# A two-layer streaming encoder on one core: the first loads and copies laid out by hand, and the q, k, v products with two token blocks at a time

## The chip, the cores and the metric

The kernel runs on one core of one Trainium2 chip. The metric is the device time of one execution in microseconds (us), as a median over runs. The engines of the core are TensorE (PE in the profile: matrix products, PEld its weight loads), VectorE (DVE), ScalarE (ACT), GpSimd (POOL) and SyncE (SP), whose queue issues nearly all DMA transfers here.

## The reference

The input x has 2048 frames of 1024 channels, everything is float32. Layer 0 is a pooling mixer, layer 1 an attention layer that reads keys and values made from layer 0's output:

```python
h = rms_norm(x, a_norm)
u, z = split(h @ a_w_in)                       # 1024 + 1024 channels
pooled = trailing means of u over 2/4/8/16 frames (4 groups of 256 channels) - u
mixed = einsum(pooled, a_w_group) * a_scale    # a 256 x 256 map per group
x = x + (mixed * silu(z)) @ a_w_out
x = x + (p[0] @ ple_w[0]) * sigmoid(x @ ple_gate_w[0])
k, v = split(rms_norm(x, kv_norm) @ w_kv);  k = rms_norm per head
q, z = split(rms_norm(x, b_norm) @ b_w_in); q = rms_norm per head
a = strictly causal stick-breaking weights of q.k / 8 (16 heads of 64)
x = x + ((a @ v) * silu(z)) @ b_w_out
x = x + (p[1] @ ple_w[1]) * sigmoid(x @ ple_gate_w[1])
```

## The kernel before

Channels lie on the 128 partitions, frames along the free axis. The 2048 frames are four chunks (0 to 3) of 512; 1024 channels are 8 tiles (KT). A float32 value is kept as a high part `hi` (rounded to the type that TensorE multiplies) and a low part `lo` (the rest), and each product takes three matmuls: hi·hi, hi·lo, lo·hi. The high part is a copy by ScalarE, the low part a subtraction by VectorE or POOL (`split`, `put_split`).

**Weights.** All weights pass through one ring of 9 buffers of 512 KB (`UNITS`, tile `wpair`) in the order of a list, `plan`. `take` hands pieces to a product, `give_back` frees the oldest buffer and calls `pump`, which starts the next load. In chunk 0 a piece comes raw (tile `wraw`, ring `io` of 4 buffers), is split, and for most weights also written to DRAM as a finished pair (`once`); later chunks load that pair (`wpair<-once`, line 156). The map of a group is folded into the input weights once: `fold(g)` multiplies the transposed weights of u (tiles `uraw`, split into `uh` and `ul`) with the group's map (`wg`) in 48 matmuls and writes the result as `wf`.

**Order of the work.** The code is written in program order; a scheduler that simulates times sets the order of instructions on each engine and of DMA issues in SP's queue. `keep_in_program_order` fixes an instruction's place; in the attention part (`state["hold"]`) TensorE's are all fixed.

**The start** (end of the function). Issued in this order: the gain `g_a`, the load of `wg` for group 3, the four `uraw` loads of group 3, eight loads of x by turns on SP's and ScalarE's queue, the z weights, five small gains on ScalarE's queue; then `fold(3)`, then `prep(0)`, which splits x (tiles `xp`) and sums the squares of x per token with 32 one-column matmuls (tile `pst`).

**A chunk.** `mixer` (z and u products per group, pooling on VectorE, tiles `mp`), `out_steps` (output projection; `xr` is product plus residual), `gate_steps`, then the products for q, k and v (`kvq`, once for each half `b` of the heads, six per chunk) and z of layer 1. In `kvq` the tokens are on the output's partitions: a product has 4 blocks `j` of 128 tokens, each 8 steps `kt` of 3 matmuls, and needs all 8 weight pieces from its first block on. A PSUM bank (two with tag `psd`) collects a block; ScalarE empties it in `valued` (tile `vr`) or `keyed` (`qs`). For v the rows are also copied shifted by one frame (`vs<-vr`, `ve<-vr`), subtracted (`differences`) and written as `vd`; for q and k transposed parts are written as `qd` and `kd` at four places of the next product, through the list `lag`. Attention over the finished chunks runs between the steps of the next chunk's products; its tiles are `qa`, `qb`, `kk`, `vv`, `pp`, `at`.

Of the kernel before, what the change touches and what calls it, by code (L numbers as in the profile page):

```python
# [11 lines left out]
AF = mybir.ActivationFunctionType  # L12
ALU = mybir.AluOpType
# [18 lines left out]
def f(ap):  # L32
    return ap.bitcast(F32)
# [3 lines left out]
def trunk_kernel(ctx, tc, x, p, a_norm, wu_t, wz_a, w_group, a_scale, a_w_out, kv_norm, w_kv,  # L37
                 k_norm, b_norm, b_w_q, b_w_z, b_q_norm, b_w_out, ple_a, ple_b, gate_a, gate_b, out):
    nc = tc.nc
    V, A, G = nc.vector, nc.scalar, nc.gpsimd  # L40
    state = {"solo": True, "hold": False, "turn": 0, "lo": 0}

# [80 lines left out]
    def rsqrt_mean(out_ap, ss, n, tag):  # L123
# [3 lines left out]
        G.tensor_tensor(out=out_ap, in0=ms, in1=neghalf[:, 0:w], op=ALU.pow)  # L127

    def split(pr, src, lo):
        A.copy(out=pr[:, 0], in_=src)  # L130
        lo.tensor_tensor(out=pr[:, 1], in0=src, in1=f(pr[:, 0]), op=ALU.subtract)
# [4 lines left out]
    plan = []  # L136
    wq = {"out": 0, "back": 0, "cap": 1, "by": nc.scalar}
    held = deque()

    def put_split(pr, raw, kts, gain):  # L140
        if gain is None:
            A.copy(out=pr[:, 0], in_=raw)  # L142
            state["lo"] += 1
            (G if state["lo"] % 3 else V).tensor_tensor(out=pr[:, 1], in0=raw, in1=f(pr[:, 0]), op=ALU.subtract)  # L144
            return
        for i, kt in enumerate(kts):
            g = gain[:, kt : kt + 1]
            A.activation(out=pr[:, 0, i], in_=raw[:, i], func=AF.Identity, scale=g)
            V.scalar_tensor_tensor(out=pr[:, 1, i], in0=raw[:, i], scalar=g, in1=f(pr[:, 0, i]),
                                   op0=ALU.mult, op1=ALU.subtract)  # L150

    def unit(key, src, kts, n, gain, keep):
        kk = len(kts)
        pr = pool.tile([P, 2, kk, n], F32R, tag="wpair", name="wpair", bufs=UNITS)
        if key in once:
            nc.sync.dma_start(out=f(pr), in_=once[key])
            return pr, kts
        raw = io("wraw").rearrange("q (k n) -> q k n", k=kk)
        wq["by"].dma_start(out=raw, in_=src[:, kts[0] : kts[-1] + 1])
        put_split(pr, raw, kts, gain)  # L160
        if keep:
            once[key] = scratch(f"once{len(once)}", [P, 2, kk, n])
            nc.sync.dma_start(out=once[key], in_=f(pr))
        return pr, kts
# [102 lines left out]
    def fold_load(g):  # L267
        maps[g] = parts = {}
        raws = {}
        for h in range(2):  # L270
            for c in range(2):
                raws[c, h] = io("uraw")
                nc.sync.dma_start(out=raws[c, h], in_=wu_t[2 * g + c, :, h * W5 : (h + 1) * W5])
        for h in range(2):
            for c in range(2):
                hi, lo = ppt("uh", F32R), ppt("ul", F32R)
                A.copy(out=hi, in_=raws[c, h])
                V.tensor_tensor(out=lo, in0=raws[c, h], in1=f(hi), op=ALU.subtract)
                parts[c, h] = (hi, lo)

    def fold(g):
        parts = maps.pop(g)
        (wg, _), = take(1)
        for kts in PAIRS:
# [9 lines left out]
            for e, kt in enumerate(kts):  # L294
                gn = g_a[:, kt : kt + 1]
                A.activation(out=pr[:, 0, e], in_=ps[:, e], func=AF.Identity, scale=gn)
                V.scalar_tensor_tensor(out=pr[:, 1, e], in0=ps[:, e], scalar=gn, in1=f(pr[:, 0, e]),
                                       op0=ALU.mult, op1=ALU.subtract)
            assert plan[wq["out"]][0] == ("wf", g, kts) and wq["out"] - wq["back"] < UNITS
# [39 lines left out]

    first_x = []  # L340

    def load_first():
        for o in range(KT):
            xin = (qryt, ppt, keyt, valt)[(0, 2, 0, 3, 0, 2, 0, 3)[o]]("xin", F32)
            (nc.sync, nc.scalar)[o % 2].dma_start(out=xin, in_=x[o * P : (o + 1) * P, 0:W5])
            first_x.append(xin)

    def prep(s):
        ck = chunk[s]
        ck["x"] = []  # L350
        for o in range(KT):
            if s:
                xin = io("xin")
                nc.sync.dma_start(out=xin, in_=x[o * P : (o + 1) * P, s * W5 : (s + 1) * W5])
            else:
                xin = first_x[o]
            pr = pair("xp")
            split(pr, xin, G if s else V)
            ck["x"].append(pr)
            if s:  # L360
                gather_squares(ck, "acc1", o, xin)
            else:
                if o == KT - 1:
                    sums = turned()
                    for i in range(KT):
                        sq = tmp("sq")
                        A.activation(out=sq, in_=first_x[i], func=AF.Square)
                        for j in range(4):
                            tc.keep_in_program_order(
                                T.matmul(sums[:, 0, j : j + 1], sq[:, j * P : (j + 1) * P], ones,  # L370
                                         start=(i + j == 0), stop=(i == KT - 1 and j == 3)))
            yield
        r = token_norm(ck["acc1"], "x") if s else rooted(sums, "x")
        yield
        ck["rb1"] = bcast(r, "x")
        yield
# [10 lines left out]
    def pooled(s, o, ps, zr):  # L387
# [21 lines left out]
        pr = pair("mp")  # L409
        split(pr, po, G)  # L410
        ck["m"][o] = pr
# [80 lines left out]
    def settle():  # L492
        while late:
            late.pop(0)()

    def kvq(s, kind, b):
        ck = chunk[s]
        us = take(KT)
        for j in range(4):
            tk = slice(j * P, (j + 1) * P)  # L500
            ps = dense()
            for kt in range(KT):
                u = us[kt][0]
                for xh, wh in ((0, 0), (1, 0), (0, 1)):
                    T.matmul(ps, ck["x2"][kt][:, xh, tk], u[:, wh, 0], start=(kt == 0 and xh == wh),
                             stop=(kt == KT - 1 and wh == 1))
                    if j == 3 and wh:
                        give_back()
                    yield
                if lag and (j, kt) in ((1, 2), (1, 5), (2, 1), (2, 4)):  # L510
                    lag.pop(0)()
            if "r2" not in ck:
                ck["r2"] = token_norm(ck["acc2"], "y")
            rj = ck["r2"][:, j : j + 1]
            settle()
            (valued if kind == "v" else keyed)(s, kind, b, j, ps, rj)

# [300 lines left out]

    nc.scalar.dma_start(out=g_a, in_=a_norm)
    pump()  # L820
    fold_load(3)
    load_first()
    wq["by"] = nc.sync
    wq["cap"] = UNITS
    pump()
    for dst, v in ((g_s, a_scale), (g_b, b_norm), (g_kv, kv_norm), (gs[:, 0:1], k_norm), (gs[:, 1:2], b_q_norm)):
        nc.scalar.dma_start(out=dst, in_=v)
    V.scalar_tensor_tensor(out=gqk, in0=gs[:, 1:2], scalar=HD ** -0.5, in1=gs[:, 0:1],
                           op0=ALU.mult, op1=ALU.mult)
    for _ in fold(3):  # L830
        pass
    for _ in prep(0):
        pass

    until((0, 0))
# [111 lines left out]
```

## Time and profile before

| what | value |
|---|---|
| median of 3 runs | 2834.18 us (2833.43 to 2836.98) |
| profiled execution | 2834.65 us, of which the span from first to last instruction is 2832.9 us |
| TensorE busy | 2733.4 us (96%), mean granted clock 0.985 |
| VectorE, ScalarE, POOL busy | 65%, 45%, 31% |
| DMA | 643.37 MB, mean 227 GB/s |

In the lists of waits below, a line gives the engine that waited, its tile and line, what it waited for, and then the sum in us, the number of times and the longest. In a list by time, a line gives start and length in us, engine, line, operation, `out<-in`, shapes and count; brackets give the idle time before it and what ended it. In a list of windows, a line gives the window, its length, the busy time of each engine with its instructions, the granted clock of TensorE, the DMA engines' busy share and GB/s.

### The profile page before, as it was taken

Reading aid. Unit: us, or ns where it says so; the run is one execution under the profiler, and the core shown is the slowest. Engines: PE = TensorE matmul, PEld = TensorE weight load, DVE = VectorE, ACT = ScalarE, POOL = GpSimd, SP = SyncE. Lnnn points to the kernel's source line nnn. Section 1 sums busy time; section 2 is a strip of 40 time slices with the busy share of each in tenths; the row PEclk is TensorE's granted clock in tenths of the full one; section 3 lists DMA queues with packets and bytes.
Section 4 is the critical chain, followed back from the end, with each engine's and each line's share of the span. In section 5 each row is a group of like instructions: output and inputs, shape, how many; then the busy total and the mean of one; then the engine's idle time right before and its main releaser. Section 6 shows DMA issues by size and latency. Waiting matters only on the chain.

```text
span 2832.9 us, 38130 instructions
## 1 busy us (share of the span) xinstructions
PE 2733.4 (96%) x13400; PEld 2246.7 (79%) x13400; DVE 1840.4 (65%) x2369; ACT 1271.2 (45%) x2496; POOL 870.4 (31%) x699
## 2 busy tenths in 40 slices
PE   7999979999988999999999999999999999999999
PEld 7888857878866787788778888888888888888777
DVE  5645444655334686766458888776777877777872
ACT  4435542344433445545344456554454444444441
POOL 1354422455423354553213434221211101111002
PEclk8999989999999999999999999999999999999999
DMA  5647899556788966786776444778577667656535
GB/s 213 222 142 278 309 323 307 178 176 208 257 258 282 334 224 218 235 308 228 244 251 219 146 147 153 241 225 274 177 230 240 244 213 255 207 198 230 176 127 185
DMA packets 306123, 643.37 MB, mean 227 GB/s; under 512 B 48646, under 2 KB 81414, under 8 KB 305932
## 3 DMA queue, kind: packets, MB, share of 16 engines
q1 hardware_dynamic: 304348, 639.62, 68.1%
q8 instruction: 105, 1.72, 0.3%
q10 hardware_dynamic: 1584, 1.33, 0.1%
q14 instruction: 86, 0.70, 0.1%
HBM read 471.43 MB, written 161.02 MB: 223 GB/s over the span
## 4 chain that ended last, share of the span: by engine, by line
PE 79%; DMA 8%; DVE 5%; SPq 2%; issue 2%; ACT 2%; POOL 2%; ACTq 0%; DVEq 0%; POOLq 0%
PE psd L46 55%; PE psl L46 8%; PE pso L46 7%; PE psa L50 7%; DMA wpair<-once 3%; DVE pp L743 2%; DVE at L760 1%; DMA wraw<-in_b_w_q_dram 1%; PE pst L50 1%; DMA xin<-in_x_dram 1%; DMA vs<-vr 1%; POOL wpair L144 1%; PE pst L46 1%; SPq L523 1%; DMA kraw<-in_b_w_out_dram 1%
## 5 line engine op out<-in xcount | busy, mean ns | idle before, releaser
L743 DVE TENSOR_TENSOR_SCAN pp<-pp,floor 128x512 f32<-128x512 f32 (+3 forms) x640 | 774.7, 1210 | 34.5 <-ACT pp L739 33.6
L760 DVE TENSOR_TENSOR at<-psa,at 128x512 fp32r<-128x512 f32 (+3 forms) x640 | 387.1, 605 | 431.9 <-ACT at L758 429.6
L46 PE MATMUL psd<-wpair,x 128*128 128x512 f32 x2304 | 620.5, 403 | 38.8 <-DMA wpair<-once 22.7
L758 ACT CAST at<-psa 128x512 fp32r<-128x512 f32 (+3 forms) x640 | 333.6, 521 | 690.6 <-PE psa L50 665.4
L46 PE MATMUL psd<-x,wpair 128*128 128x512 f32 x2304 | 599.3, 393 | 3.5 <-ACT sg L481 3.5
L46 PEld LDWEIGHTS psd<-wpair,x 128*128 128x128 f32 x2304 | 426.0, 191 | 139.6 <-DMA wpair<-once 38.0
L46 PEld LDWEIGHTS psd<-x,wpair 128*128 128x128 f32 x2304 | 427.0, 188 | 92.5 <-ACT sg L481 4.6
L46 PE MATMUL psd<-xp,wpair 128*128 128x512 f32 x1536 | 391.8, 396 | 6.4 <-DMA wpair<-once 6.4
L50 PE MATMUL psa<-ident,pp 128*128 128x128 f32 x2176 | 347.2, 274 | 17.4 <-DVE pp L743 6.6
L46 PE MATMUL pso<-at,vv 128*128 128x512 f32 (+3 forms) x1280 | 361.5, 364 | 0.2 <-DVE at L760 0.2
L50 PEld LDWEIGHTS psa<-ident,pp 128*128 128x128 f32 x2176 | 274.8, 141 | 104.8 <-DVE at L760 12.2
L739 ACT ACTIVATE pp<-psl 128x512 f32<-128x512 f32 (+3 forms) x640 | 344.6, 538 | 12.5 <-PE psl L46 9.2
L46 PEld LDWEIGHTS psd<-xp,wpair 128*128 128x128 f32 x1536 | 287.4, 190 | 66.3 <-DMA wpair<-once 7.7
L46 PE MATMUL psl<-kk,qa 128*128 128x512 f32 (+3 forms) x640 | 284.4, 444 | 2.9 <-DMA kk<-kd 2.9
L46 PEld LDWEIGHTS pso<-at,vv 128*128 128x128 f32 x1280 | 240.7, 189 | 54.0 <-DVE at L760 0.5
L46 PE MATMUL psl<-kk,qb 128*128 128x512 f32 (+3 forms) x640 | 234.2, 366 | 0.0
L46 PE MATMUL psd<-og,wpair 128*128 128x512 f32 x744 | 202.6, 395 | 2.0 <-DVE os L773 2.0
L46 PE MATMUL psd<-mp,wpair 128*128 128x512 f32 x768 | 196.9, 398 | 7.5 <-DVE xr L449 7.5
L144 POOL TENSOR_TENSOR wpair<-wraw,wpair 128x512 fp32r<-128x512 f32 x101 | 148.4, 1474 | 128.3 <-ACT wpair L142 127.9
L46 PEld LDWEIGHTS psd<-mp,wpair 128*128 128x128 f32 x768 | 145.0, 192 | 38.2 <-DVE xr L449 8.3
L46 PEld LDWEIGHTS psd<-og,wpair 128*128 128x128 f32 x744 | 137.5, 188 | 31.5 <-DVE os L773 2.6
L474 POOL TENSOR_TENSOR xj<-x 128x512 f32<-128x512 f32 x64 | 101.7, 1594 | 135.5 <-DVE sg L485 129.6
(112 smaller groups left out, 2747.4 us busy)
## 6 DMA issues: line engine op xcount, KB each, us to landing
wpair<-once SPq DMA_DIRECT2D x384, 512.0 KB
once<-wpair SPq DMA_DIRECT2D x80, 512.0 KB
kk<-kd SPq DMA_DIRECT2D x160, 256.0 KB
vv<-vd SPq DMA_DIRECT2D x160, 256.0 KB
wpair<-wf SPq DMA_DIRECT2D x48, 512.0 KB
once<-kp SPq DMA_DIRECT2D x36, 512.0 KB
wraw<-in_a_w_out_dram SPq DMA_DIRECT2D x64, 256.0 KB
wraw<-in_gate_a_dram SPq DMA_DIRECT2D x64, 256.0 KB
```

Source lines behind the costliest of these rows:

```text
L46: return held_in_order(nc.tensor.matmul(*a, **k))
L50: return held_in_order(nc.tensor.transpose(*a, **k))
L144: (G if state["lo"] % 3 else V).tensor_tensor(out=pr[:, 1], in0=raw, in1=f(pr[:, 0]), op=ALU.subtract)
L474: G.tensor_tensor(out=xj, in0=f(x1[o][:, 0]), in1=f(x1[o][:, 1]), op=ALU.add)
L523: nc.sync.dma_start(out=vs[lo + 1 : hi + 1], in_=vr[lo:hi])
L739: A.activation(out=pp[:, r0:], in_=ps[:, :w], func=AF.Sigmoid, scale=-1.0)
L743: V.tensor_tensor_scan(out=pp[:, r0:][:, ::-1], data0=pp[:, r0:][:, ::-1], data1=least, initial=1.0 if st["diag"] else st["carry"][j], op0 ...
L758: A.copy(out=at[:, 0, cs], in_=pt[:, cs])
L760: return lambda: V.tensor_tensor(out=at[:, 1, cs], in0=pt[:, cs], in1=f(at[:, 0, cs]), op=ALU.subtract)
```

## The change

1. **The start** is a function of its own, `boot`. The first two of four map pieces are loaded first, on two queues (into `t4` tiles `u`, two pieces each, not the `io` ring), then `wg`, the other two pieces, then `g_a` and x; seven of x's eight loads and the five small gains are on SP's queue. Copies and subtractions of the start are fixed in program order (`booted`); the splits of the first z weights wait in a list `later` and are called at set places. Half of x's low parts go from VectorE to POOL. The whole fold of group 3 is issued in pieces of 12 or 13 matmuls between the copies, and the sums of squares come after 56 of the xp products.
2. **`kvq`** walks the list `STEPS`: blocks 0 and 1 as before, then block 2 alone for four steps, then blocks 3 and 2 by turns, then block 3's last four steps. The weight piece of a step is still given back by block 3.
3. **`pooled`**: the low parts of `mp` for channel tiles 0 and 1 (the group that comes last) are made by VectorE instead of POOL.

```diff
-            A.activation(out=pr[:, 0, i], in_=raw[:, i], func=AF.Identity, scale=g)
...
+            booted(A.activation(out=pr[:, 0, i], in_=raw[:, i], func=AF.Identity, scale=g))
...
-        wq["by"].dma_start(out=raw, in_=src[:, kts[0] : kts[-1] + 1])
-        put_split(pr, raw, kts, gain)
+        booted(nc.sync.dma_start(out=raw, in_=src[:, kts[0] : kts[-1] + 1]))
+
+        def finish():
+            put_split(pr, raw, kts, gain)
+            if keep:
+                nc.sync.dma_start(out=once[key], in_=f(pr))
+
...
+        if state["boot"]:
+            later.append(finish)
+        else:
+            finish()
...
     def load_first():
+        two = [t4("u0") for _ in range(2)]
+        for h in range(2):
+            for c in range(2):
+                first_u[c, h] = f(two[h])[:, c]
+                ins = (nc.scalar if c else nc.sync).dma_start(out=first_u[c, h],
+                                                             in_=wu_t[6 + c, :, h * W5 : (h + 1) * W5])
+                if not c:
+                    booted(ins)
+            if h == 0:
+                pump()
+        nc.scalar.dma_start(out=g_a, in_=a_norm)
...
-            (nc.sync, nc.scalar)[o % 2].dma_start(out=xin, in_=x[o * P : (o + 1) * P, 0:W5])
+            ins = (nc.scalar if o == 1 else nc.sync).dma_start(out=xin, in_=x[o * P : (o + 1) * P, 0:W5])
...
+    def cast_first(os):
+        for o in os:
+            pr = pair("xp")
+            booted(A.copy(out=pr[:, 0], in_=first_x[o]))
+            booted((G if o % 2 else V).tensor_tensor(out=pr[:, 1], in0=first_x[o], in1=f(pr[:, 0]), op=ALU.subtract))
...
+    def boot():
+        load_first()
+        later.pop(0)()
+        fold_split(3, first_u)
+        wq["cap"] = UNITS
+        pump()
+        run = fold(3)
...
+        cast_first(range(4))
+        folds(13)
+        cast_first(range(4, KT))
+        folds(12)
+        later.pop(0)()
+        folds(12)
+        later.pop(0)()
+        later.pop(0)()
+        folds(12)
+        later.pop(0)()
+        sum_first()
...
-        split(pr, po, G)
+        split(pr, po, G if o > 1 else V)
...
+    STEPS = [(j, kt) for j in range(2) for kt in range(KT)]
+    STEPS += [(2, 0), (2, 1), (2, 2), (2, 3), (3, 0), (2, 4), (3, 1), (2, 5), (3, 2), (2, 6), (3, 3), (2, 7)]
+    STEPS += [(3, kt) for kt in range(4, KT)]
+
     def kvq(s, kind, b):
...
-        for j in range(4):
+        banks = {}
+        for j, kt in STEPS:
             tk = slice(j * P, (j + 1) * P)
-            ps = dense()
-            for kt in range(KT):
-                u = us[kt][0]
...
+            if kt == 0:
+                banks[j] = dense()
+            u = us[kt][0]
+            for xh, wh in ((0, 0), (1, 0), (0, 1)):
+                T.matmul(banks[j], ck["x2"][kt][:, xh, tk], u[:, wh, 0], start=(kt == 0 and xh == wh),
+                         stop=(kt == KT - 1 and wh == 1))
+                if j == 3 and wh:
+                    give_back()
+                yield
```

How the rows of two engines change at the start. First SP's queue, from its first row on, before (xin is x, uraw a map piece, wraw of in_wz_a a z weight piece):

```order
L345 DMA xin<-in_x_dram 128x512 x2
L273 DMA uraw<-in_wu_t_dram 128x512 x3
L345 DMA xin<-in_x_dram 128x512 x2
L273 DMA uraw<-in_wu_t_dram 128x512
L159 DMA wraw<-in_wz_a_dram 128x512 x4
```

and after (u_379 and u_380 are the two tiles of the map pieces):

```order
L363 DMA u_379<-in_wu_t_dram 128x512
L164 DMA wraw<-in_a_w_group_dram 128x512
L363 DMA u_380<-in_wu_t_dram 128x512
L372 DMA xin<-in_x_dram 128x512 x7
L164 DMA wraw<-in_wz_a_dram 128x512 x4
L421 DMA gains<-in_a_scale_dram 128x8
```

The map pieces and wg now stand ahead of x (the other two pieces are the first two rows of ScalarE's queue), and the gains behind the z weights. ScalarE's copies at the start, before (uh is the high part of a map piece, wpair<-psd the folded weights, sq the squares):

```order
L277 CAST uh<-uraw 128x512
L827 DMA gains<-in_kv_norm_dram 128x8
L827 DMA gs<-in_k_norm_dram 128x1
L827 DMA gs<-in_b_q_norm_dram 128x1
L130 CAST xp<-xin 128x512 x8
L367 ACTIVATE sq<-xin 128x512 x6
L277 CAST uh<-uraw 128x512
L148 ACTIVATE wpair<-wraw,g_a 128x256 x8
L296 ACTIVATE wpair<-psd,g_a 128x256 x7
```

and after:

```order
L147 CAST wpair<-wraw 128x512
L293 CAST uh<-u_379 128x512 x2
L293 CAST uh<-u_380 128x512 x2
L380 CAST xp<-xin 128x512 x4
L312 ACTIVATE wpair<-psd,g_a 128x256 x2
L380 CAST xp<-xin 128x512 x4
L312 ACTIVATE wpair<-psd,g_a 128x256 x2
L153 ACTIVATE wpair<-wraw,g_a 128x256 x2
L312 ACTIVATE wpair<-psd,g_a 128x256 x2
L153 ACTIVATE wpair<-wraw,g_a 128x256 x4
L312 ACTIVATE wpair<-psd,g_a 128x256 x2
L153 ACTIVATE wpair<-wraw,g_a 128x256 x2
```

The fourth map piece moved from behind x and the squares to the front, and the folded and z weights are copied by turns. On TensorE, behind the fold of group 3, before:

```order
L46 MATMUL psd<-wpair,ul 128x256
L46 MATMUL pst<-ones,sq 128x1 x32
L46 MATMUL psd<-xp,wpair 128x512 x22
L50 MATMUL pst<-ident,r 128x128 x4
L46 MATMUL psd<-xp,wpair 128x512 x70
```

and after:

```order
L46 MATMUL psd<-wpair,uh 128x256
L46 MATMUL psd<-xp,wpair 128x512 x56
L46 MATMUL pst<-ones,sq 128x1 x32
L46 MATMUL psd<-xp,wpair 128x512 x22
L50 MATMUL pst<-ident,r 128x128 x4
L46 MATMUL psd<-xp,wpair 128x512 x18
```

The sums of squares stand behind 56 of the 96 xp matmuls (before, behind four that stood within the fold). The second place is SP's queue in chunk 1 at the end of the first v product, where the loads for the next q product (`wpair<-once`) stand. Before:

```order
L571 DMA kd_7_316<-hl 64x2x512
L540 DMA vd_0_359<-vv 128x8x128
L523 DMA vs<-vr 112x512
L523 DMA vs<-vr 15x512
L530 DMA ve_0_367<-vr 1x512
L156 DMA wpair<-once_3573 128x1024
L156 DMA wpair<-once_3583 128x1024
L156 DMA wpair<-once_3593 128x1024
L156 DMA wpair<-once_3603 128x1024
```

and after:

```order
L643 DMA kd_7_316<-hl 64x2x512
L161 DMA wpair<-once_3558 128x1024
L161 DMA wpair<-once_3571 128x1024
L161 DMA wpair<-once_3584 128x1024
L612 DMA vd_0_359<-vv 128x8x128
L595 DMA vs<-vr 112x512
L595 DMA vs<-vr 15x512
L602 DMA ve_0_367<-vr 1x512
L161 DMA wpair<-once_3609 128x1024
```

Three of the eight loads moved ahead of vd, vs and ve (one more stands ahead of the four kd rows). TensorE's own rows are the same number in both, 13342.

107 lines of the change are left out of this document (52 added, 55 removed).

## The prediction

> **What bounds the kernel now.** I read the page first, then the list of waits of TensorE, then its gaps in order of time, and last what each gap waits for.
>
> ```profile
> span 2832.9 us, 38130 instructions
> PE 2733.4 (96%) x13400; PEld 2246.7 (79%) x13400; DVE 1840.4 (65%) x2369; ACT 1271.2 (45%) x2496; POOL 870.4 (31%) x699
> PE psd L46 <- DMA wpair<-once: 29.1, 28, 7.2
> PE psd L46 <- ACT uh L277: 14.2, 2, 8.1
> PE psd L46 <- ACT wpair L148: 13.6, 5, 6.1
> ```
>
> TensorE works 96% of the span, so what can be won without touching its matmuls is its idle time, 2832.9 − 2733.4 = 99.5 us, and the time in which its clock is low. Three entries are weights that were late (29.1 and 13.6 us) or the first pieces of the map (14.2 us at the start). The stages with the late weights are the last parts of the chunks, where the q, k, v products run; one row per chunk (each engine's busy time, then granted clock, DMA share, GB/s):
>
> ```profile
> 350.00:490.00 140.00, 117.47 (x517) 92.77 (x516) 61.56 (x91) 51.35 (x92) 32.50 (x31) 0.90 0.95 315
> 805.00:945.00 140.00, 121.23 (x564) 95.88 (x563) 57.28 (x81) 53.42 (x109) 40.86 (x37) 0.94 0.85 281
> 1330.00:1470.00 140.00, 132.35 (x648) 104.82 (x647) 72.64 (x99) 59.18 (x119) 31.77 (x30) 0.99 0.75 238
> 1925.00:2065.00 140.00, 138.82 (x714) 114.70 (x712) 100.11 (x123) 67.30 (x134) 30.34 (x25) 1.00 0.66 217
> ```
>
> TensorE is idle 22.5, 18.8, 7.6 and 1.2 us there; the DMA engines are full in chunk 0, have 15% left in chunk 1 and 25% in chunk 2. So the price of late weights sits in chunks 0 and 1, and only chunk 0 has no room in its transfers.
>
> **Part 1, the start.** TensorE's order of time at the start, and what ScalarE and SP's queue do meanwhile:
>
> ```profile
> 8.14 0.79 PE L46 MATMUL psd<-wpair,uh 128*128 128x256 f32 x2 [8.14 <-ACT uh L277]
> 9.25 0.41 PE L46 MATMUL psd<-wpair,uh 128*128 128x256 f32 x1
> 9.46 0.41 PE L46 MATMUL psd<-wpair,ul 128*128 128x256 f32 x1
> 14.76 0.28 PE L46 MATMUL psd<-wpair,ul 128*128 128x256 f32 x1
> 14.88 0.28 PE L46 MATMUL psd<-wpair,uh 128*128 128x256 f32 x1
> 21.23 0.80 PE L46 MATMUL psd<-wpair,uh 128*128 128x256 f32 x2 [6.07 <-ACT uh L277]
> 26.00 11.64 PE L46 MATMUL pst<-ones,sq 128*128 128x1 f32 x64
> 37.49 7.29 PE L46 MATMUL psd<-xp,wpair 128*128 128x512 f32 x22
> 44.98 16.14 PE L46 MATMUL psd<-xp,wpair 128*128 128x512 f32 x70
> 60.95 0.28 PE L46 MATMUL psd<-wpair,uh 128*128 128x256 f32 x1
> 61.00:350.00 289.00, 289.00 (x1360) 1.00 0.66 232
> 13.28 4.26 ACT L130 CAST xp<-xin 128x512 fp32r<-128x512 f32 x8 [2.84 <-DMA gains<-in_a_scale_dram]
> 20.58 0.60 ACT L277 CAST uh<-uraw 128x512 fp32r<-128x512 f32 x1
> 21.09 2.50 ACT L148 ACTIVATE wpair<-wraw,g_a 128x256 fp32r<-128x256 f32 x6
> 9.87 12.39 SPq L159 DMA_DIRECT2D wraw<-in_wz_a_dram  x4
> GB/s 0 0 104 267 241 295 279 391 388 382 410 393 336 352 347 321 342 369 249 144 8 0 0 11 0 0 0 0 0 0 79 295 363 292 284 412 399 402 404 388
> ```
>
> The fold of group 3 (48 matmuls) stops after 25 for 6.07 us: its fourth raw piece was cast at 20.58, behind the eight casts of x (13.28 to 17.54) and the squares of x. The last row is the DMA rate from 0 to 30 us in slices of 0.75 us: nothing moves from 15.75 to 22.5, since the z weights (9.87, four issues in 12.39 us) wait for buffers. Both are order, not work.
>
> The common milestone is the first matmul of the next fold, at 60.95; ahead of it both versions have 48 fold matmuls, 96 of xp, 32 sums (64 records) and 4 transposes. After the change:
> - The first four transfers are two map pieces, wg and the third piece, 4 x 0.26 = 1.05 MB. The slices sum to 0.89 MB at 5.25 and 1.18 at 6.0, so they are there at 5.65; the casts of wg and of one piece (0.60 each) put the first matmul at 6.9.
> - ScalarE, by the order: wg, 4 pieces, 4 x, 2 wf, 4 x, 2 wf, then the first z piece. A 512-wide cast goes each 4.26 / 8 = 0.53, a 256-wide one each 2.50 / 6 = 0.42: 5.65 + 0.6 + 12 x 0.53 + 5 x 0.42 = 14.7. x is no limit: 3.4 MB are in by 12.
> - The fold: starts of matmuls lie 0.21 us apart at 9.25 and 0.12 at 14.76, so TensorE's clock was half for some 6.2 us. As before, 28 slow ones take 6.0 and 20 fast ones 2.4: end at 15.3. For the lo parts that VectorE and POOL make I add 0.7: xp starts at 16.0.
> - One xp matmul is (60.95 − 44.98) / 70 = 0.228. By the order 56, the sums, 22, transposes and 18: 16.0 + 12.8 + 11.5 (26.00 to 37.49) + 7.5 (37.49 to 44.98, with transposes) + 4.1 = 51.9.
>
> That is 60.95 − 51.9 = 9.0 us less. Low end 6: TensorE waits for the second to fourth z piece (their casts alternate with wf casts that wait for VectorE). High end 10.4: the clock opens after 3.2 us, as it did from 21.23 on. The Trainium skill (TensorE: Matmul & The Clock Gate, Part 1) says that the clock is full after about 3.4 us of sustained matmuls, whenever they begin; by it the fold ends some 1.3 us sooner and the sum is 1.3 us lower. The second burst agrees with it and the first does not, so I leave that outside the sum. From 61 to 350 us TensorE is busy without a gap (289.00 of 289.00), so the 9.0 us reach chunk 0's end; weights are fetched when TensorE gives a buffer back, so that distance moves along. The five gain loads leave ScalarE's queue (they held its casts 2.84 us) for SP's, behind the z weights; the first user of them comes after 60 us, so that is free. The DMA pause moves to nothing: the wf and once writes (8 x 0.5 MB) follow at once, and the next fold's pieces are behind them as before.
>
> **Part 2, two token blocks together.** Before, block 3 gave weights back at its steps, 9 to 16 of the 16 that blocks 2 and 3 take; now at steps 5, 7, 9, 11 and 13 to 16. The first comes 4 steps sooner, then 3, 2, 1, 0.
>
> ```profile
> 286.38 27.37 PE L46 MATMUL psd<-wpair,x 128*128 128x512 f32 x120
> 819.32 3.33 SPq L571 DMA_DIRECT2D kd<-hl  x4
> 822.75 0.70 SPq L540 DMA_DIRECT2D vd<-vv  x1
> 823.50 3.36 SPq L523 DMA_DIRECT2D vs<-vr  x2
> 827.43 4.06 SPq L156 DMA_DIRECT2D wpair<-once  x8
> 831.34 2.30 PE L46 MATMUL psd<-wpair,x 128*128 128x512 f32 x4 [7.20 <-DMA wpair<-once]
> 899.40 3.36 PE L46 MATMUL psd<-wpair,x 128*128 128x512 f32 x7 [5.11 <-DMA wpair<-once]
> PE psd L46 <- DMA wpair<-once: 20.9, 18, 7.2
> PE psd L46 <- DMA wpair<-once: 4.4, 9, 0.7
> ```
>
> A step is 3 matmuls of 27.37 / 120 = 0.228, 0.68 us, and about 0.85 where attention runs between: 2.7 to 3.4 us sooner. It works through SP's queue. The wait of 7.20 is no lack of bytes: eight weight loads stood behind vd and two vs copies and issued at 827.43. By the order three of them now stand ahead of vd, one ahead of kd: 827.43 − 822.75 = 4.7 us sooner.
> - Chunk 1 (the list of waits from 760 to 945 us, first of the two): 20.9 us. 7.20 loses 4.7; the one of 5.11 loses 3.4; the rest, 8.6 in sixteen small waits, lies mostly inside that advance, say 6.4: 14.5 at best. Loads that come sooner queue with other traffic at 0.85 share, so I take 9; ends 4 and 14.5.
> - Chunk 2 (the second, 1330 to 1470): 4.4 us in nine waits under 0.7. I take 3, ends 1 and 4.4. Chunk 3: nothing.
> - Chunk 0: 22.5 us, but at 0.95 share the room is 0.05 x 140 = 7 us. I take 3, ends 0 and 7.
> - Clock. After a long gap it is half until TensorE has run some time:
>
> ```profile
> 826.00:827.00 1.00, 0.00 (x0) 0.96 1.03 290
> 837.00:838.00 1.00, 1.00 (x6) 0.92 1.00 356
> 830.40 0.62 ACT L538 CAST vv<-vs 128x512 fp32r<-128x512 f32 x1 [6.19 <-POOL vs L535]
> 1064.88 2.03 POOL L131 TENSOR_TENSOR mp<-us,mp 128x512 fp32r<-128x512 f32 x1 [2.19 <-ACT mp L130]
> 1075.15 0.66 DVE L449 TENSOR_TENSOR xr<-psd,xr 128x512 f32<-128x512 f32 x1
> 1075.86 1.47 PE L46 MATMUL psd<-mp,wpair 128*128 128x512 f32 x3 [4.19 <-DVE xr L449]
> ```
>
>   It fell just before 827, where TensorE had stopped at 831.34 − 7.20 = 824.1, and came back just after 837: of the work from 831.34 on some 5.8 us ran at half, 2.9 us lost. If the gap of 5.11 costs as much, cutting both below 2.5 us wins 5.8 at best; I take 3, since I leave 2.5 of the one and 1.7 of the other.
> - New waits. A PSUM bank of the pair is wanted again 4 steps after its block ends (2.7 us) instead of 8 (5.5), and ScalarE, which empties it, can stand behind a vv cast for 6.19 us. I take 2 lost; ends 0 and 8.
>
> Sum: 9 + 3 + 3 + 3 − 2 = 16 gained.
>
> **Part 3, the low parts.** Eight subtractions (o of 0 and 1 in four chunks) go from POOL (2.03 in the row) to VectorE at about the 0.66 of a 512-wide one. No matmul waits for the POOL one: it ended at 1066.9, and the gap at 1075.86 is for the bank that the xr add frees, which stands behind VectorE's queue. So nothing is gained and one 0.6 is added there: 0.6 lost, ends 0 and 1.3.
>
> **Sum.** 2834.65 (the profiled execution, 0.5 above the median of 2834.18) − 9.0 − 16 + 0.6 = 2810.2; I say 2810.
>
> **Rivals.**
> - Traffic takes it back: loads start sooner but land as late, since chunk 0 is at 0.95 and chunk 1 in stretches at 1.0. Chunk 0 gives 0, chunk 1 gives 3, chunk 2 gives 1, clock 1, new waits −3, together 2: 2834.65 − 9 − 2 + 0.6 = 2824. For it speak the shares, against it the 7.20, which is an issue held back.
> - All of part 2 comes: 7 + 14.5 + 4.4 + 5.8 = 31.7, and 2834.65 − 9 − 31.7 + 0.6 = 2794.6. Against it again the shares.
> - The start's gain is lost: the pieces of the next fold come at about 58 as before, so TensorE waits for them: 2810 + 9 = 2819. Against it: SP has their loads ahead of more of the once writes than before.
> - Slower: ScalarE empties the banks late. Each spot costs 6.19 − 2.7 = 3.5 us, 2810 + 3.5 N; there are 2 spots in each of 24 products, and the kernel is slower by 0.2% from N = 9 (2841.5). For it the row at 830.40; against it, that is a stand of ScalarE while TensorE itself was stopped, and in chunk 3 no wait of that size is seen.
>
> **How the numbers follow.** The forecast 2810 (2800 to 2820 where no term reaches its end) has 0.62, traffic 0.18, all of part 2 0.08, the start lost 0.08, slower 0.04. The range 2796 to 2826 leaves out the slower case, most of the full gain and the tails of traffic. A measurement tells 0.2% (5.7 us) from no change: faster than 2828.5 is all of four cases but a tail of traffic, 0.91; same 0.05; slower 0.04.
>
> **What would show it.** Right: first matmul near 7, no idle time over 1 us until the xp products, next fold near 52; no wait of 7 us in chunk 1, weights' waits there about 10 us, chunk 0 still near 20. Wrong: waits of TensorE for ScalarE's vr or qs at L46, a late uh in the second fold, or the idle time of chunk 1 unchanged.

## The result and the profile after

The changed kernel takes 2811.41 us (median of four runs, 2806.34 to 2817.46), the kernel before 2834.18 (2833.43 to 2836.98): a ratio of 0.9919, with 95% between 0.9898 and 0.994, so 0.6 to 1.0% faster. The forecast was 2810 us. The profiled execution is the longest of the four, 2817.46 us with a span of 2815.7; by the two profiled executions the change wins 17.2 us, by the medians 22.8. Two executions lie far above all others, one of e2_kvq (3453.95 us) and one of the kernel before (15448.73 us), and enter no figure. From the page, as before:

```profile
span 2815.7 us, 38145 instructions
PE 2733.7 (97%) x13400; PEld 2249.9 (80%) x13400; DVE 1847.9 (66%) x2373; ACT 1272.0 (45%) x2496; POOL 863.9 (31%) x695
```

TensorE's busy time is what it was (2733.4); its idle time fell from 99.5 to 82.0 us, by 17.5, which covers the difference of the spans (17.2). Its list of waits shows where:

```profile
PE psd L46 <- DMA wpair<-once: 17.5, 20, 4.8
PE psd L46 <- ACT wpair L153: 14.0, 6, 9.3
PE psd L46 <- ACT uh L293: 7.5, 2, 7.0
PE psl L46 <- DMA kk<-kd: 3.0, 1, 3.0
```

The weights fetched by DMA went from 29.1 to 17.5 us, the map pieces of the start from 14.2 to 7.5; the weights copied by ScalarE stayed (13.6 to 14.0). No wait for vr or qs is in the list. The start, in TensorE's order of time:

```profile
7.02 0.79 PE L46 MATMUL psd<-wpair,uh 128*128 128x256 f32 x2 [7.02 <-ACT uh L293]
8.41 0.80 PE L46 MATMUL psd<-wpair,ul 128*128 128x256 f32 x2 [0.59 <-DVE ul L294]
14.80 0.28 PE L46 MATMUL psd<-wpair,ul 128*128 128x256 f32 x1
16.72 12.88 PE L46 MATMUL psd<-xp,wpair 128*128 128x512 f32 x56
29.44 11.64 PE L46 MATMUL pst<-ones,sq 128*128 128x1 f32 x64
40.94 7.30 PE L46 MATMUL psd<-xp,wpair 128*128 128x512 f32 x22
52.63 0.28 PE L46 MATMUL psd<-wpair,uh 128*128 128x256 f32 x1
```

The wait of 6.07 us within the fold is gone, the xp products begin at 16.72, and the next fold at 52.63 instead of 60.95. The DMA rate of these first 30 us, in slices of 0.75 us, has no empty stretch left (the old one, from 15.75 to 22.5 us, was nine slices long, with 11 GB/s in one of them):

```profile
GB/s 0 0 55 238 341 374 404 375 365 393 246 183 232 303 341 391 366 407 399 321 164 70 266 421 22 169 421 404 393 404 421 382 399 399 399 284 238 429 426 300
```

The four stretches with the q, k, v products, one row per chunk, shifted by 10 to 17 us to begin at the same work (length, then each engine's busy time, then granted clock, DMA share, GB/s):

```profile
340.00:480.00 140.00, 120.91 (x534) 94.45 (x533) 60.99 (x90) 52.17 (x92) 34.91 (x34) 0.91 0.95 309
793.00:933.00 140.00, 127.02 (x591) 102.01 (x590) 58.55 (x83) 54.91 (x111) 40.68 (x37) 0.94 0.88 289
1315.00:1455.00 140.00, 135.11 (x672) 109.30 (x672) 76.68 (x105) 62.15 (x123) 35.14 (x33) 0.99 0.77 245
1908.00:2048.00 140.00, 139.61 (x719) 115.60 (x717) 101.10 (x123) 66.81 (x134) 30.91 (x26) 1.00 0.65 210
```

TensorE is idle 19.1, 13.0, 4.9 and 0.4 us there, against 22.5, 18.8, 7.6 and 1.2. The DMA share rose in chunk 1 from 0.85 to 0.88, the rate from 281 to 289 GB/s: more bytes in the same 140 us. In chunk 1 the wait of 7.20 us is gone; first TensorE's stops of over 1 us between 800 and 900 us, then the rows of SP's queue that belong to them:

```profile
816.19 0.50 PE L46 MATMUL psd<-wpair,x 128*128 128x512 f32 x1 [3.15 <-DMA wpair<-once]
822.86 1.11 PE L46 MATMUL psd<-wpair,x 128*128 128x512 f32 x3 [2.07 <-DMA wpair<-once]
825.15 1.22 PE L46 MATMUL psd<-wpair,x 128*128 128x512 f32 x2 [1.18 <-DMA wpair<-once]
885.89 2.38 PE L46 MATMUL psd<-wpair,x 128*128 128x512 f32 x4 [4.76 <-DMA wpair<-once]
811.11 1.82 SPq L161 DMA_DIRECT2D wpair<-once  x3
813.02 0.38 SPq L612 DMA_DIRECT2D vd<-vv  x1
813.50 2.64 SPq L595 DMA_DIRECT2D vs<-vr  x2
816.70 2.72 SPq L161 DMA_DIRECT2D wpair<-once  x4
```

Of the eight loads that had issued together at 827.43, behind vd and two vs rows, three now issue at 811.11, ahead of them, and four at 816.70. The one stop of 7.20 us became three, 3.15 + 2.07 + 1.18 = 6.4 us in all, so little was won at this place.

### The profile page after: what moved, and what is told of

Same layout as the page of the kernel before. It is cut to its first block, busy times and chain, and to the rows that moved or that the text cites. A ratio compares the mean times of both kernels' runs of the same rounds, so it can differ in the third digit from the quotient of the medians.

```text
span 2815.7 us, 38145 instructions
## 1 busy us (share of the span) xinstructions
PE 2733.7 (97%) x13400; PEld 2249.9 (80%) x13400; DVE 1847.9 (66%) x2373; ACT 1272.0 (45%) x2496; POOL 863.9 (31%) x695
## 4 chain that ended last, share of the span: by engine, by line
PE 77%; DMA 9%; DVE 6%; issue 2%; SPq 2%; POOL 2%; ACT 2%; ACTq 0%; DVEq 0%; POOLq 0%
PE psd L46 53%; PE pso L46 8%; PE psl L46 8%; PE psa L50 7%; DMA wpair<-once 2%; DVE pp L815 2%; DMA vs<-vr 2%; DVE at L832 1%; DMA wraw<-in_gate_a_dram 1%; PE pst L50 1%; DMA wraw<-in_w_kv_dram 1%; DVE wpair L154 1%; DMA wraw<-in_b_w_q_dram 1%; PE pst L46 1%; SPq L595 0%
## 5 line engine op out<-in xcount | busy, mean ns | idle before, releaser
L50 PE MATMUL psa<-ident,pp 128*128 128x128 f32 x2176 | 346.8, 274 | 14.2 <-DVE pp L815 5.7
L46 PEld LDWEIGHTS psd<-mp,wpair 128*128 128x128 f32 x768 | 145.4, 192 | 38.1 <-DVE xr L514 7.7
```

Of the source, the lines that this page charges most:

```text
L46: return held_in_order(nc.tensor.matmul(*a, **k))
L50: return held_in_order(nc.tensor.transpose(*a, **k))
```

## The experiments

For the sake of one table, TensorE's time is cut at five points of the work: the start of the next fold, the first product with mp in chunks 1, 2 and 3, the first product with og, and the span's end. Each column is the length of a piece in one profiled execution (us), read from the first rows of these products in TensorE's order of time:

| kernel | to the fold | chunk 0 | chunk 1 | chunk 2 | chunk 3 | the rest |
|---|---|---|---|---|---|---|
| before | 60.95 | 504.1 | 491.9 | 572.5 | 492.3 | 711.2 |
| e3_low | 57.2 | 504.8 | 494.6 | 571.8 | 492.9 | 711.2 |
| e1_start | 49.9 | 506.6 | 492.3 | 571.0 | 492.5 | 710.8 |
| e2_kvq | 61.6 | 500.4 | 485.2 | 573.0 | 491.9 | 711.9 |
| after | 52.6 | 501.5 | 486.9 | 571.9 | 491.3 | 711.5 |
| e4_start_kvq | 48.5 | 498.3 | 484.0 | 573.1 | 491.5 | 711.0 |
| e8_free | 49.6 | 498.4 | 485.5 | 572.3 | 491.7 | 711.1 |
| e6_vs_act | 48.9 | 499.3 | 486.4 | 572.4 | 493.3 | 711.3 |
| e10_offset6 | 48.7 | 497.9 | 490.1 | 574.1 | 496.3 | 710.7 |
| e7_offset2 | 49.6 | 492.0 | 480.8 | 568.8 | 489.8 | 711.9 |
| e9_offset1 | 49.6 | 495.2 | 486.2 | 568.3 | 489.0 | 711.8 |
| e5_sums_dve | 38.9 | 504.1 | 484.8 | 572.7 | 489.6 | 712.5 |
| e11_offset2_sums | 38.1 | 497.3 | 483.9 | 570.3 | 489.3 | 714.0 |
| e12_offset1_sums | 38.3 | 496.9 | 485.7 | 567.0 | 488.1 | 713.9 |

Times are compared by their ratio to the kernel before, run beside them on the same chip (its median was 2834.18 for the changed kernel, 2835.98 to 2836.57 for the experiments); brackets hold 95%.

### The parts one by one

**e1_start** has the new start alone: `kvq` and `pooled` are those of before.

```diff
-        split(pr, po, G if o > 1 else V)
+        split(pr, po, G)
...
-        for j, kt in STEPS:
...
+        for j in range(4):
...
```

> The start laid out by hand, with kvq and the low parts as before. Prediction's sum: 9 us less than before, 2825, with the next fold's first matmul at 52 to 53 us and the gaps of chunks 0 and 1 as before (about 22 and 21 us). Rival (the start's gain is taken back by the transfers of chunk 0): next fold at 52 to 53, but the first gap of chunk 0 grows by what was won, and the time is 2832 to 2835.

2824.75 us, 0.9955 [0.9943, 0.9967], as the prediction's sum said. **e2_kvq** is the kernel before with the walk over `STEPS` alone:

```diff
...
-        for j in range(4):
...
+        for j, kt in STEPS:
...
```

> Only the walk over STEPS in kvq, start and low parts as before. Prediction's sum: 16 us less, 2818, with some 9 us fewer of waits for weights in chunk 1. By the profile of the changed kernel (chunk 0 2.6, chunk 1 4.8, chunk 2 0.4 us between its landmarks): 8 us less, 2826. Rival (traffic takes it back): 2 us less, 2832, with the gaps in other places.

2826.58 us, 0.9959 [0.9946, 0.9972]: the 2826 read off the changed kernel's profile, not the 2818 of the prediction's sum. **e3_low** is the kernel before with the low parts on VectorE alone:

```diff
-        split(pr, po, G)
+        split(pr, po, G if o > 1 else V)
```

> Only the low parts of the last group by VectorE. Prediction's sum: 0.6 us more, 2834.8, the gap ahead of the xr add in chunk 2 longer by about 0.6. Rival (POOL's queue was in the way of something): 1 to 4 us less, with the xr gaps of 3.3 and 4.2 us shorter.

2836.99 us against 2836.57, 0.9999 [0.9991, 1.0008]: nothing, with an interval that leaves at most 2.6 us of gain and 2.3 of loss. **e4_start_kvq** is the changed kernel without the low parts:

```diff
-        split(pr, po, G if o > 1 else V)
+        split(pr, po, G)
```

> The whole change but the low parts, which stay with POOL. If the parts add up, this is the changed kernel less 0.6 us: 2811; if the low parts carry some of the gain, 2812 to 2816.

2810.8 us, 0.9909 [0.9895, 0.9922], no different from the whole change (0.9919 [0.9898, 0.994]). The start is worth 0.45% (12.8 us of 2836.57), the steps 0.41% (11.6), both together 0.91% (25.8): the parts add up, so neither gives back what the other wins.

### Is it the order written by hand, or the room?

**e8_free** is the changed kernel in which nothing at the start is fixed in program order; the loads, the tiles and the queues stay.

```diff
     def booted(ins):
-        if state["boot"]:
-            tc.keep_in_program_order(ins)
+        return ins
```

> The changed kernel without the fixed places in program order at the start (the same loads, tiles and queues, ordered by the scheduler). If the resources (map pieces out of the io ring) carry the start's gain: within 3 us of the changed kernel. If the hand order does: the casts of x come ahead of the pieces again, next fold near 58, and 6 to 9 us above the changed kernel, 2819.

2809.42 us, 0.9901 [0.9887, 0.9914], and the next fold begins at 49.6. So the fixed order adds nothing that can be seen. What wins at the start lies in what this kernel keeps, the map pieces' own tiles, the order of the loads and the queues; these were not tried one by one.

### When a weight buffer comes back

The steps' gain could be the moment at which buffers are given back, or what the paired blocks do elsewhere. Three kernels change only how many steps block 3 runs behind block 2 (8 is before, 4 the change). In the diff the first new line is that of e7_offset2, the second that of e10_offset6:

```diff
-    STEPS += [(2, 0), (2, 1), (2, 2), (2, 3), (3, 0), (2, 4), (3, 1), (2, 5), (3, 2), (2, 6), (3, 3), (2, 7)]
-    STEPS += [(3, kt) for kt in range(4, KT)]
+    STEPS += [(2, 0), (2, 1), (3, 0), (2, 2), (3, 1), (2, 3), (3, 2), (2, 4), (3, 3), (2, 5), (3, 4), (2, 6), (3, 5), (2, 7), (3, 6), (3, 7)]
...
+    STEPS += [(2, 0), (2, 1), (2, 2), (2, 3), (2, 4), (2, 5), (3, 0), (2, 6), (3, 1), (2, 7), (3, 2), (3, 3), (3, 4), (3, 5), (3, 6), (3, 7)]
```

> The changed kernel, with block 3 two steps behind block 2 instead of four (weights given back at steps 3, 5, 7, 9, 11, 13, 15, 16 of 16). If the moment of giving back sets the waits: 3 to 6 us below the changed kernel, 2806. If SP's queue or the transfers set them: within 2 us of it. If a bank that is not yet empty holds block 3: waits of TensorE for vr or qs at the block's start, and 5 us or more above.

> The changed kernel with block 3 six steps behind block 2 (weights given back at steps 7, 9, then 11 to 16 as in the product before). If the gain follows the moment of the first pieces evenly: half way between the start alone (2825) and the changed kernel (2811), 2818. If only the order of SP's queue counts and it is already that of four steps: 2811. If the first pieces have to come some 4 steps sooner at all: 2825.

**e9_offset1** lets the two blocks alternate from the first step, (2,0) (3,0) (2,1) (3,1) and so on:

> The changed kernel with block 3 one step behind block 2 (weights given back at steps 2, 4, 6, 8, 10, 12, 14, 16). With 8, 4 and 2 steps behind, the chunks 0 to 2 took 1570, 1560 and 1542 us from the second fold to chunk 3's mixer. Theory (the moment of giving back sets the waits): a little below two steps behind, 2789 to 2794. Rival (the bank of block 1 is not yet empty when block 3 begins): TensorE waits for vr or qs in each product, and the time is at or above that of two steps, 2794 to 2805.

With the new start in all of them (e1_start also has the low parts on POOL, which e3_low shows to be worth nothing):

| block 3 behind block 2 by | buffers come sooner (steps, all eight together) | median, us | ratio to before |
|---|---|---|---|
| 8 steps (e1_start) | 0 | 2824.75 | 0.9955 [0.9943, 0.9967] |
| 6 steps (e10_offset6) | 3 | 2818.77 | 0.9936 [0.9923, 0.995] |
| 4 steps (the change) | 10 | 2811.41 | 0.9919 [0.9898, 0.994] |
| 2 steps (e7_offset2) | 21 | 2794.05 | 0.9853 [0.9839, 0.9866] |
| 1 step (e9_offset1) | 28 | 2801.89 | 0.9888 [0.9872, 0.9905] |

The sooner the buffers come, the shorter the kernel, down to two steps. The step from 4 to 2 wins 0.66% and that from 8 to 4 won 0.36%; but e4_start_kvq and e8_free, which have four steps too, lie at 0.9909 and 0.9901, and with them the two gains can't be told apart. Six steps came out at the 2818 of their even case. Two steps went far past the best case expected (2806), and one step missed its 2789 to 2794. The order holds for the whole time and not for each chunk: in the table above six steps are as short as four in chunk 0 (497.9), and lose in chunk 1 (490.1) and chunk 3 (496.3). A rival stays open. Block 2 ends later the closer block 3 follows (at step 8, 10, 12, 14 and 15 of the 16), and with it move its copies and their rows in SP's queue; no kernel moves the one without the other. That the moment of giving back is the cause is argued from the order of these times, not shown alone.

The forecast's limit, that full DMA engines leave chunk 0 some 3 us, doesn't hold: chunk 0 takes 492.0 us in e7_offset2, 13 less than without the steps (504.1 to 506.6), and the forecast's upper end was 7. Its list of waits alone would not tell why:

```profile
PE psd L46 <- DMA wpair<-once: 16.7, 12, 4.2
PE psd L46 <- ACT wpair L153: 10.9, 2, 10.1
PE psd L46 <- ACT qs L616: 0.4, 1, 0.4
```

27.6 us of waits for weights against 31.5, but in 14 waits instead of 26. The rest is clock. One row for the piece up to chunk 1 and one for the next, first of before, then of after, then of e7_offset2 (length, busy time of TensorE and the others, granted clock, DMA share, GB/s):

```profile
60.95:565.00 504.05, 481.52 (x2230) 397.54 (x2229) 276.65 (x401) 206.58 (x380) 197.81 (x174) 0.97 0.73 249
565.00:1056.90 491.90, 466.48 (x2208) 378.96 (x2208) 263.43 (x345) 203.96 (x413) 209.09 (x172) 0.98 0.75 250
```

```profile
52.63:554.10 501.47, 481.60 (x2231) 396.16 (x2230) 282.65 (x407) 206.65 (x380) 196.60 (x176) 0.98 0.73 249
554.10:1041.00 486.90, 466.60 (x2209) 380.64 (x2208) 265.28 (x347) 203.84 (x413) 206.81 (x170) 0.98 0.76 252
```

```profile
49.64:541.60 491.96, 475.68 (x2230) 394.21 (x2229) 282.26 (x407) 207.60 (x380) 198.73 (x176) 0.99 0.74 254
541.60:1022.40 480.80, 464.46 (x2208) 380.14 (x2207) 267.33 (x347) 204.04 (x413) 207.43 (x170) 0.98 0.77 255
```

The same 2230 matmuls of chunk 0 keep TensorE busy 475.7 us in e7_offset2 and 481.6 in the changed kernel, since the clock falls once instead of three times there (what it lacks to 1, summed over windows of 1 us, is 6.8 us against 12.0). Summed over windows of 1 us from the start to the end, what the granted clock lacks to 1 is 41.0 us before, 41.0 after, and 30.7 in e7_offset2. Between before and after the clock's part is nothing and the idle time (99.5 to 82.0) all. Between after and e7_offset2 the idle time fell by 8.3 (to 73.7) and the clock's part by 10.3, together 18.6 of the 22.8 us between these two spans (2815.7 and 2792.9); the rest lies in TensorE's busy time (2733.7 and 2719.2) and isn't assigned.

At one step the forecast's other side appears: waits of TensorE for a bank that ScalarE has not emptied.

```profile
PE psd L46 <- ACT qs L616: 3.6, 4, 1.4
PE psd L46 <- ACT vr L591: 1.4, 2, 1.2
```

That is 5.0 us where two steps have 0.4, and e9_offset1 is 0.35% (9.9 us) above e7_offset2. But these waits replace others: TensorE's idle time is 74.2 us in all against 73.7, and what the clock lacks 29.0 against 30.7. The difference of the two spans (7.2 us) lies in its busy time (2725.9 against 2719.2), which no view here takes apart.

### SP's queue alone

**e6_vs_act** is the changed kernel in which the vs and ve copies, three or four per block of a v product, issue on ScalarE's queue instead of SP's, so that no weight load stands behind those copies.

```diff
-            nc.sync.dma_start(out=vs[lo + 1 : hi + 1], in_=vr[lo:hi])
+            nc.scalar.dma_start(out=vs[lo + 1 : hi + 1], in_=vr[lo:hi])
...
-        nc.sync.dma_start(out=ve[s][b][j : j + 1], in_=vr[P - 1 : P])
+        nc.scalar.dma_start(out=ve[s][b][j : j + 1], in_=vr[P - 1 : P])
```

> The changed kernel, with the shifted copies of v (vs, ve) issued on ScalarE's queue instead of SP's. Theory (weights of chunks 0 and 1 are late because their issues stand behind others in SP's queue): the waits for weights of chunk 0 and 1 (16 and 15 us) fall to a third, the time 10 to 15 us below the changed kernel, 2796 to 2801. Rival (the transfers themselves are full): those waits stay within 4 us of where they are, the time 2808 to 2812; or ScalarE's issues hold its copies and the time is above 2815.

2814.76 us, 0.9924 [0.9911, 0.9937], the same as the change's 0.9919. The waits for weights do fall, but little, and a wait for qs comes in:

```profile
PE psd L46 <- DMA wpair<-once: 16.7, 19, 4.5
PE psd L46 <- ACT wpair L153: 10.2, 4, 4.5
PE pst L50 <- DVE qs L624: 3.0, 1, 3.0
```

At the place of the old wait of 7.20 us the stops of TensorE are 0.91 and 2.74 us, 3.65 where four profiles with four steps have 5.1 to 6.6; which speaks for the vs rows holding loads back there. But the kernel isn't faster for it: the wait for qs comes in, and chunk 1 takes 486.4 us where those four take 484.0 to 486.9. The theory (2796 to 2801) is wrong. The vs and ve rows ahead of the loads aren't what is left to win.

### The sums of squares, and the fastest version

At the start the squares of x are summed on TensorE by 32 matmuls of one column (64 records). **e5_sums_dve** is the changed kernel in which VectorE adds the eight squares and four such matmuls sum the result:

```diff
-        sums = turned()
-        for i in range(KT):
+        acc = pool.tile([P, W5], F32, tag="acc", name="acc", bufs=1)
+        booted(A.activation(out=acc, in_=first_x[0], func=AF.Square))
+        for i in range(1, KT):
             sq = tmp("sq")
...
-            for j in range(4):
-                tc.keep_in_program_order(
-                    T.matmul(sums[:, 0, j : j + 1], sq[:, j * P : (j + 1) * P], ones,
-                             start=(i + j == 0), stop=(i == KT - 1 and j == 3)))
-        chunk[0]["rb1"] = bcast(rooted(sums, "x"), "x")
+            booted(V.tensor_tensor(out=acc, in0=acc, in1=sq, op=ALU.add))
+        chunk[0]["rb1"] = bcast(token_norm(acc, "x"), "x")
```

> The changed kernel, with the squares of the first x added by VectorE and 4 one-column matmuls in place of 32. Theory (TensorE's clock falls during the one-column matmuls, at a moment that varies from run to run, and this costs their 9 to 11.6 us and the slow matmuls behind them): next fold at 40 to 42 instead of 48.5 to 52.6 us, the granted clock at 1.00 from 15 to 60 us, the time 9 to 12 us below the changed kernel, 2799 to 2802. Rival (the sums fill time in which the next fold's pieces are not there yet): the next fold's first matmul still near 49, the time 2809 to 2812.

2803.54 us, 0.9882 [0.9867, 0.9897]; the next fold begins at 38.91, some ten us sooner, as the theory said. **e11_offset2_sums** and **e12_offset1_sums** join this with two steps and with one step between the blocks.

> Two steps behind, and the sums of squares by VectorE. If the two gains add (16 and 7 us below the changed kernel): 2787. If chunk 0's transfers take the sums' gain back: 2792 to 2794.

> One step behind, and the sums of squares by VectorE: by the same sum, 7 us below the kernel with one step behind. Rival as there: banks that are not empty, and a time at or above two steps with these sums.

e11_offset2_sums: 2792.85 us, 0.9845 [0.983, 0.986], the lowest of all and 0.7% below the changed kernel. But e7_offset2 has 0.9853 without the sums, within its interval: the second case of the expectation came, and the 11.5 us of the start are nearly all given back. The table shows where: 5.3 us in chunk 0, 3.1 in chunk 1, 1.5 in chunk 2, 2.1 in the rest. In chunk 0 most of it is clock (nearly the same matmuls, 2228, are busy 479.4 us instead of 475.7; the window begins behind the fold's first two matmuls, at 38.90 instead of 38.11):

```profile
38.90:535.40 496.50, 479.37 (x2228) 396.21 (x2227) 283.32 (x413) 212.54 (x387) 201.44 (x177) 0.98 0.74 256
```

e12_offset1_sums: 2793.15 us, 0.9851 [0.9835, 0.9866], the same as e11, though it has the waits for qs (3.1 us) and vr (1.5) that e9_offset1 has. So these waits don't by themselves make one step worse than two; why e9_offset1 lost 0.35% stays open. With one step the sums win 0.37% (0.9888 to 0.9851), so the three fastest kernels (e7, e11, e12) meet at 2793 to 2794 us, and what holds them there is open too.

## Why the prediction was right, term by term

Four profiles have the steps at an offset of 4 and everything else close (after, e2_kvq, e4_start_kvq, e8_free), three don't have them (before, e1_start, e3_low); for the start it is three against three. The means of the table's columns, gains above zero:

| term | forecast | measured | how |
|---|---|---|---|
| start | 9.0 (6 to 10.4) | 8.3 in the pair of profiles; 9.6 | 60.95, 61.6, 57.2 against 52.6, 49.9, 48.5 |
| steps, chunk 0 | 3 | 5.5 | 505.1 against 499.7 |
| steps, chunk 1, with clock and new waits | 9 + 3 − 2 | 7.5 | 492.9 against 485.4 |
| steps, chunk 2 | 3 | −0.8 | 571.8 against 572.6 |
| steps, chunk 3 | 0 | 1.0 | 492.6 against 491.6 |
| low parts | −0.6 | 0 (−2.3 to 2.6) | e3_low |

9.6 + 5.5 + 7.5 − 0.8 + 1.0 is 22.8, which is the difference of the medians (the last column of the table, for the rest, would take 0.3 off again). The parts are right in kind, the start and the weights that come sooner. That the sum of 24.4 came out so near is partly luck: chunk 0 gave 2.5 more than I had taken, chunk 1 2.5 and chunk 2 3.8 less.

- **The start** went as worked out: first matmul 7.02 (forecast 6.9), xp from 16.72 (16.0), next fold at 52.63 (51.9). That this one trace agrees within 0.8 us is luck in part: it is the slowest of the seven profiles with this start and these sums, the others have the next fold at 48.5 to 49.9, since their sums took 8.9 to 9.6 us and not the 11.5 that I had taken. By e1_start's ratio the start is worth 12.8 us (9.4 to 16.2), above my high end of 10.4, with an interval that holds it. TensorE's first burst ran at half until 14.80, 7.8 us after 7.02 instead of the 6.2 I had taken. (The old fold stopped after 30 of its 48 matmuls, by the rows up to 14.88, not after 25 as I had counted; the sum does not use this.) The step on ScalarE was wrong in what it named: I gave the low end to late z pieces. The first one is split at 17.73, three us later than I had it, and cost nothing, since the 56 xp products begin with the folded weights. ScalarE's rows show why it was late:

```profile
10.62 0.62 ACT L380 CAST xp<-xin 128x512 fp32r<-128x512 f32 x1 [1.05 <-DMA xin<-in_x_dram]
17.35 0.47 ACT L312 ACTIVATE wpair<-psd,g_a 128x256 fp32r<-128x256 f32 x1 [0.93 <-DVE wpair L313]
17.73 0.90 ACT L153 ACTIVATE wpair<-wraw,g_a 128x256 fp32r<-128x256 f32 x2
```

  "x is no limit" was false by 1.8 us (two waits, 1.05 and 0.72), and each pair of folded weights waited for VectorE.
- **Chunk 1** won 6.1 of the 20.9 us of waits for weights (14.8 are left; I had said about 10 left), but not where I had put them. Of the wait of 7.20, 4.7 us were to go; three of together 6.4 are left, 0.8 less. The three loads that moved ahead issue 5.4 us sooner, counted from the chunk's first product with mp (554.09 after, 565.05 before): 257.0 us behind it instead of 262.4. The four behind vd and vs issue at 262.6, no sooner than before, and the waits are for them too. In e2_kvq, e4_start_kvq and e8_free this place costs 5.1, 5.5 and 6.6 us, in e1_start and e3_low 8.9 and 9.7, so the means fall by 2.7 us. Of the wait of 5.11, 3.4 us were to go; it became 4.76. The first of its loads issue some 6 us sooner by the same count, but the block of the last only 1.3 us (324.1 against 325.4), first before, then after:

```profile
890.42 6.03 SPq L156 DMA_DIRECT2D wpair<-once  x6
878.18 5.14 SPq L161 DMA_DIRECT2D wpair<-once  x5
```

  So the last loads hardly issued sooner, though by the order of the steps their buffers came back sooner; ahead of them in SP's queue stand the same two qd rows and a once row as before, and the DMA engines are full in both (1.02 in the window of 896 before, 1.10 in that of 882 after). Which of these holds them was not tried. What was won are the sixteen small waits, 8.6 us in all, of which 3.7 are left. The term for chunk 1 came near its size because I had cut it down for traffic, not because the long waits went as worked out. The clock's 3 us didn't come either: it fell at both places again. Windows of 1 us after (TensorE's busy time, clock, DMA share, GB/s):

```profile
817.00:818.00 1.00, 1.00 (x5) 0.50 0.93 362
824.00:825.00 1.00, 0.00 (x0) 0.50 1.00 397
888.00:889.00 1.00, 1.00 (x6) 0.50 1.03 418
1474.00:1475.00 1.00, 1.00 (x4) 0.50 0.99 385
```

  One stop of 7.20 made one fall; stops of 3.15 and 2.07 make two, and what the clock lacks there is 5.1 us both times. The Trainium skill (TensorE: Matmul & The Clock Gate, Part 1) has the clock go back to half after about 3.4 us without work. Here it was at half at 817 and at 824, behind stops of 3.15 and 2.07 us, so by this trace shorter ones do. Not each of them: in the kernel before, a stop of 2.29 us ahead of 2067.10 left it at 1.00, so the length of a stop alone doesn't tell.
- **Chunk 2** gained 2.1 us of waits for weights (4.4 to 2.3), as said, and lost them to a wait that I had not named:

```profile
1471.48 0.47 PE L46 MATMUL psl<-kk,qa 128*128 128x512 f32 x1 [3.01 <-DMA kk<-kd]
```

  It brings the clock down (the window at 1474 above). In e2_kvq the same matmul waits 3.2 us, and in e4_start_kvq and e8_free it stops as long at the same place, where the lists put it down to ScalarE's sg:

```profile
PE psl L46 <- ACT sg L448: 3.0, 1, 3.0
PE psl L46 <- ACT sg L447: 3.4, 1, 3.4
```

  Without the steps this place costs 0.7 us at most (e1_start), with two steps or one nothing over 0.2. With four steps it took back what chunk 2 won. In e6_vs_act, which has four steps and other rows in SP's queue, it isn't there, so it hangs on that queue's order too. Before, a wait for kd of this size (2.9 us) lay in chunk 0; there 0.4 is left.
- **Chunk 0** won more than I had taken. In the means TensorE's waits for weights split by ScalarE fall from 15.2 to 12.9 us, those for loaded weights from 3.3 to 0.6, that for kd from 2.4 to 0.1. The room that I had worked out from a mean share of 0.95 over 140 us was no limit: e7_offset2 wins some 8 us more there (499.7 to 492.0), with a share of 0.74 over the whole piece.
- **New waits** for banks: none at four steps, so the 2 us were too much; 0.4 us at two steps.
- **The low parts**: nothing that can be seen, as near to the 0.6 us as the noise allows.
- **The rivals.** Traffic taking it all back (2824) is excluded by e2_kvq, 11.6 us won with 95% from 7.9 to 15.3. That everything comes (2794.6) is what two steps give (2794.05), by another way. The start wasn't lost: e1_start keeps it to the end. The kernel isn't slower. Banks emptied late appear first at one step, with 5.0 us.

## What to carry to other kernels

When prefetched buffers are what TensorE waits for, try two or three distances between giving a buffer back and needing it again before anything else: here the best was two steps off the one chosen and 0.5 to 0.7% better, while moving other rows out of the queue that refills the buffers gained nothing (e6_vs_act). A sum of waits is not their whole price: the changed kernel and e7_offset2 wait nearly as long for weights (31.5 and 27.6 us) and differ by 10.3 us in clock. Their number doesn't tell it either: e1_start has 40 such waits and the clock lacks 37.5 us, the changed kernel has 26 and lacks 41.0. And what is won at the start must be followed to the end, since a start some ten us sooner was worth 5 to 10 us with four steps (0.9901 to 0.9919 against 0.9882), 10 with one (0.9888 to 0.9851) and about 2, inside the noise, with two (0.9853 to 0.9845).

## What the runs showed of the hardware

TensorE's clock falls during matmuls of one column, though the profile shows it busy all the time. Windows of 1 us in the changed kernel; the sums begin at 29.44:

```profile
29.00:30.00 1.00, 1.00 (x9) 1.00 0.97 334
31.00:32.00 1.00, 1.00 (x10) 0.82 0.77 289
32.00:33.00 1.00, 1.00 (x6) 0.50 0.11 39
44.00:45.00 1.00, 1.00 (x4) 0.50 0.56 213
45.00:46.00 1.00, 1.00 (x5) 0.85 0.00 0
```

It stays at half until 45, four us into the xp products behind them. In e5_sums_dve, where four such matmuls stand in place of 32, it stays at 1.00 until 346 us. The moment of the fall differs between executions of the same instructions, and so does the length of the sums (first e3_low, then e4_start_kvq; 11.64 in the two profiles before and after):

```profile
25.42 8.84 PE L46 MATMUL pst<-ones,sq 128*128 128x1 f32 x64
28.57 9.03 PE L46 MATMUL pst<-ones,sq 128*128 128x1 f32 x64
```

From the start of the sums to the next fold it is 23.2 us in the changed kernel and 20.0 in e4_start_kvq, 35.0 before and 31.7 in e3_low. So this alone moves the start by some three us from run to run, as much as some terms of the forecast; one pair of profiles can't settle a term of that size, and the means above are over three and four.
